# Spacing the blocks of the channel sub-layer's matmul operands 32 bytes further apart

## Chip, core and metric

The kernel runs on one core of a Trainium2 chip. The metric is the device time of one execution in microseconds (us). Before the change the median of three runs is 1179.09 us (1177.92 to 1179.61).

## What is computed

One layer of an encoder: a mixer sub-layer (neighbourhood attention and a two-way state-space branch), then the channel sub-layer, each followed by a layer norm. The change touches the channel sub-layer alone, which is a two-layer perceptron with a squared ReLU on 512 tokens, 1024 channels and 4096 hidden channels:

```python
def sq_relu_mlp(x, w1, w2):
    return jnp.square(jax.nn.relu(x @ w1)) @ w2

# in reference():
    h = layer_norm(DN_ALPHA * h + mix, ln1_g[l], ln1_b[l])
    h = layer_norm(DN_ALPHA * h + sq_relu_mlp(h, w_ff1[l], w_ff2[l]), ln2_g[l], ln2_b[l])
```

All data are float32.

## The kernel before

Every large product is done in three matmuls. Each operand is split into a rounded high part and the remainder (names ending in `h` and `l`), both of type float32r, and `mm3` (lines 404 to 406) adds high x high, low x high and high x low into one PSUM bank. A matmul has a **stationary** operand of 128 columns, which is loaded into the array as "weights", and a **moving** operand of 512 or 256 columns, which is streamed through. In the profile's names `ps_f<-h1Th,wh_f` the first name behind the arrow is the moving operand, the second the stationary one; the load of the stationary operand is a record of its own (PEld).

The channel sub-layer works on the hidden channels in four quarters of 1024 (`NQ`), each as eight tiles of 128 (`f`).

- **First product** (`ff1_half`, line 1458, and `ff1_tile`, line 1660). Moving: the normed tokens, transposed, as two tiles `h1Th` and `h1Tl` of eight blocks of 512 columns, one block for each 128 input channels. Stationary: a slab of `w_ff1` of 256 hidden channels, as eight blocks of 256 columns. For each of the eight blocks k there are three matmuls, with moving `h1Th`, `h1Th`, `h1Tl` of block k. The first four tiles of quarter 0 are done in two token halves (moving 256 columns, 192 matmuls in all), interleaved with the transposes that make `h1T`; their slabs are asked for with `shift=16`, that is 16 floats or 64 bytes into the tile (line 1500). All other tiles of the four quarters are 512 wide: 96 matmuls in quarter 0 and 192 in each other quarter, 672 in all.
- **Second product of quarters 0 to 2** (`ff2_strassen`, line 1561): 504 matmuls of 512 columns by Strassen's scheme. Its weights come by DMAs that add to what lies in the buffer (`w2r`, line 1570), and are split by ScalarE (line 1575) and VectorE (line 1576). Its operands are not moved by the change.
- **Second product of quarter 3** (`ff2`, line 1552). Stationary: the squares `gh` and `gl`, again eight blocks of 512 columns. Moving: blocks of 512 weights; 168 matmuls of 512 columns, and at the very end 48 of 256.

Slabs and split weights rotate through three pairs of buffers: two pairs of 2112 floats in pool `wp`, cut by `wide` (line 391), and one pair of 2048 floats in pool `w3` (`third`), cut by its own shape. `parts` (line 1522) deals them out in turn. `squares` (line 1687) makes the tiles of 4096 floats for the squares; `gh` and `gl` take the buffers of the first two quarters' squares, and the weights `rest` (line 1725) the third.

Below, the **place** of a block is the byte in its partition at which it begins, modulo 256. In the built program every tile of the channel sub-layer named above begins at a multiple of 256 bytes (`h1Th` at byte 70400, `wh` of pool `wp` at 36608 and 45056), and a block of 512 or 256 floats is 2048 or 1024 bytes long. So before the change every block has place 0, except the blocks of the slabs that are asked for with `shift=16`, which have place 64. The same holds in the mixer: `ps_z` (moving `wh_z`, `wl_z`) and the first `ps_x` slabs have place 64 by a shift, and most other operands place 0.

The order on each engine comes partly from a planner (the mixer) and partly from the order in which the code is written (the channel sub-layer).

Of the kernel before, what the change touches and what calls it, by code (L numbers as in the profile page):

```python
# [11 lines left out]
F32 = mybir.dt.float32  # L12
F32R = mybir.dt.float32r
# [6 lines left out]
P = 128  # L20
S = 512
D = 1024
NT = S // P
KD = D // P
# [333 lines left out]
def encoder_layer(ctx, tc, x, w_in, w_attn_br, w_ssd_br, w_o, w_ff1, w_ff2, pcols, rows64,  # L358
# [8 lines left out]
    wp = ctx.enter_context(tc.tile_pool(name="wp", bufs=2))  # L367
# [4 lines left out]
    def split_weights(parts, nk, ncol, name, hi, lo, eng=nc.vector, pool=None, after=None):  # L372


        st = (pool or wp).tile([P, nk, ncol], F32, tag="ws", name=f"ws_{name}")
        c = 0
        for src, r0, c0, n in parts:
            nc.sync.dma_start(
                st[:, :, c : c + n],
                src[r0 : r0 + nk * P, c0 : c0 + n].rearrange("(k p) c -> p k c", p=P),  # L380
            )
            c += n
        hk = nk // 2
        for i, k in enumerate((slice(0, hk), slice(hk, nk))):
            with tc.issue_after(after[i]) if after else ExitStack():
                nc.scalar.activation(hi[:, k], st[:, k], AF.Copy)  # L386
            (eng[i] if isinstance(eng, tuple) else eng).tensor_tensor(out=lo[:, k], in0=st[:, k], in1=hi[:, k].bitcast(F32),  # L387
                              op=ALU.subtract)
        return hi, lo

    def wide(t, nk, shift=0):

        return t[:, shift : shift + 2048].rearrange("p (k c) -> p k c", k=nk)

    def weights(parts, nk, ncol, name, eng=nc.vector, pool=None, after=None, shift=0):
        if pool:
            hi, lo = [pool.tile([P, nk, ncol], F32R, tag=n, name=f"{n}_{name}") for n in ("wh", "wl")]
        else:
            hi, lo = [wide(wp.tile([P, 2112], F32R, tag=n, name=f"{n}_{name}"), nk, shift)
                      for n in ("wh", "wl")]  # L400
        return split_weights(parts, nk, ncol, name, hi, lo, eng, pool, after)

    def mm3(o, lh, ll, rh, rl, start, stop):
        nc.tensor.matmul(o, lh, rh, start=start, stop=False)  # L404
        nc.tensor.matmul(o, ll, rh, start=False, stop=False)  # L405
        return nc.tensor.matmul(o, lh, rl, start=False, stop=stop)  # L406
# [89 lines left out]
    def slab(name, parts, nk, ncol, engs, shift=0):  # L496

        ws = plan.tile(f"ws_{name}", "ws", wp, [P, nk, ncol], F32)
        wh, wl = [plan.tile(f"{n}_{name}", n, wp, [P, 2112], F32R, lambda t: wide(t, nk, shift))
                  for n in ("wh", "wl")]  # L500
        c = 0
        keys = []
        for j, (src, r0, c0, n) in enumerate(parts):
            op("SP", 4.0 * n / ncol, lambda src=src, r0=r0, c0=c0, n=n, c=c: nc.sync.dma_start(
                ws()[:, :, c : c + n],
                src[r0 : r0 + nk * P, c0 : c0 + n].rearrange("(k p) c -> p k c", p=P)),
               r=[("behind", 0)], w=[(ws.name, j)], at=4.8 if name == "x0" else 4.4)
            keys.append((ws.name, j))
            c += n
        hk = nk // 2  # L510
        for i, (k, eng) in enumerate(zip((slice(0, hk), slice(hk, nk)), engs)):
            op("ACT", 1.06, lambda k=k: nc.scalar.activation(wh()[:, k], ws()[:, k], AF.Copy),
               r=keys, w=[(wh.name, i)])
            e, us = ("DVE", 1.24) if eng is nc.vector else ("POOL", 2.42)
            on = {"D": nc.vector, "P": nc.gpsimd}.get(ON.get(f"{wl.name}.{i}"), eng)
            op(e, us, lambda k=k, on=on: on.tensor_tensor(
                out=wl()[:, k], in0=ws()[:, k], in1=wh()[:, k].bitcast(F32), op=ALU.subtract),
               r=keys + [(wh.name, i)], w=[(wl.name, i)], lock=True)
        return wh, wl
# [828 lines left out]
    for tag, n in (("qf", 1), ("kf", 1), ("kh", 2), ("klz", 2), ("qs", 2)):  # L1348
        t = atp.tile([P, n, S], F32R, tag=tag, name=f"aTl_{tag}")
# [9 lines left out]
    for d2 in range(4):  # L1359
# [3 lines left out]
        tag = ("so", "mm")[d2 % 2]  # L1363
# [79 lines left out]
    apool.__exit__(None, None, None)  # L1443
    hpool.__exit__(None, None, None)
    fp = ctx.enter_context(tc.tile_pool(name="fp", bufs=1, reuse_waits="tile"))
    h1Th = fp.tile([P, KD, S], F32R, tag="h1Th", name="h1Th")
    h1Tl = fp.tile([P, KD, S], F32R, tag="h1Tl", name="h1Tl")
    acc = [fp.tile([P, D], F32, name=f"acc{t}") for t in range(NT)]
    h0.update({t: first_norm(t, acc[t], nc.gpsimd) for t in (2, 3)})

# [7 lines left out]
    def ff1_half(w1, j, ps, half):  # L1458

        c = slice(half * 256, (half + 1) * 256)  # L1460
        for k in range(KD):
            mm3(ps[:, c], w1[0][:, k, j * P : (j + 1) * P], w1[1][:, k, j * P : (j + 1) * P],
                h1Th[:, k, c], h1Tl[:, k, c], k == 0, k == KD - 1)

    def third(pool, name, shape=[P, KD, 256]):
        return [pool.tile(shape, F32R, tag=n, name=f"{n}_{name}") for n in ("wh3", "wl3")]
# [16 lines left out]
    for t2 in range(2):  # L1483
        toks = (2 * t2, 2 * t2 + 1)
        for c in range(2):
            cs = slice(c * 512, (c + 1) * 512)
            tag = ("mm", "so")[c]
# [8 lines left out]
        if t2:  # L1496

            early = []
            for s in range(2):
                w1 = weights([(w_ff1, 0, s * 256, 256)], KD, 256, f"f1_0_{s}", shift=16)  # L1500
                for j in range(2):
                    tag = ("so", "yd", "cb", "so")[2 * s + j]
# [12 lines left out]
    ffp = ctx.enter_context(tc.tile_pool(name="ffp", bufs=1, reuse_waits="tile"))  # L1515
# [3 lines left out]
             for i in range(2)]  # L1519
    turn = {"parts": 2, "raw": 0}  # L1520

    def parts(name, shape):

        turn["parts"] += 1
        if turn["parts"] % 3 == 0:
            return third(w3p, name, shape)
        return [wide(wp.tile([P, 2112], F32R, tag=n, name=f"{n}_{name}"), shape[1])
                for n in ("wh", "wl")]

    def raw(name):  # L1530
# [130 lines left out]
    def ff1_tile(fq, f, last):  # L1661

        s, j = f // 2, f % 2
        if fq == 0 and s < 2:
            w1, ps = early[f]
            ff1_half(w1, j, ps, 1)
        else:
            if j == 0:
                slab[0] = split_weights([(w_ff1, 0, fq * D + s * 256, 256)], KD, 256, f"f1_{fq}_{s}",
                                        *parts(f"f1_{fq}_{s}", [P, KD, 256]))  # L1670
            w1 = slab[0]
            ps = psx.tile([P, S], F32, tag="mm", bufs=BANKS["mm"], name=f"ps_f1_{fq}_{f}")
            for k in range(KD):
                mm3(ps, w1[0][:, k, j * P : (j + 1) * P], w1[1][:, k, j * P : (j + 1) * P],
                    h1Th[:, k, :], h1Tl[:, k, :], k == 0, k == KD - 1)
        rl = ffp.tile([P, S], F32, tag="rl", bufs=2, name=f"rl{fq}_{f}")
        nc.scalar.activation(rl, ps, AF.Relu)
        if last:
            nc.vector.tensor_tensor(out=rl, in0=rl, in1=ps, op=ALU.mult)
            nc.scalar.activation(gh[:, f, :], rl, AF.Copy)  # L1680
            return nc.vector.tensor_tensor(out=gl[:, f, :], in0=rl, in1=gh[:, f, :].bitcast(F32),
                                           op=ALU.subtract)
        return nc.scalar.activation(r2[fq][:, f, :], rl, AF.Square)

    slab = [None]

    def squares(name, dtype=F32):
        return ffp.tile([P, KD, S], dtype, tag="r2", bufs=3, name=name)

    r2 = [squares(f"r2_{fq}") for fq in range(2)]  # L1690
    for fq in range(2):
        for f in range(KD):
            ins = ff1_tile(fq, f, False)
            if fq == 1 and f == 0:
                begin = ins
            if fq == 0 and f == 4:

                for t in range(NT):
                    for i, o in ((0, ALU.mult), (1, ALU.add)):
                        aff = nc.gpsimd.tensor_tensor(out=acc[t], in0=acc[t], in1=row1[i], op=o)  # L1700
                        if i == 0:
                            tc.add_manual_dep(aff.ins, ins.ins.name, mybir.DependencyInfo(
                                mybir.DependencyClass.Sync, mybir.DependencyReason.DATA),
                                reason="behind the first channels")

    r2.append(squares("r2_2"))
    run = ff2_strassen(0, 0, r2[:2])
    for f in range(0, KD, 2):
        for _ in range(3):
            next(run)  # L1710
        ff1_tile(2, f, False)
        ff1_tile(2, f + 1, False)
    for _ in run:
        pass

    gh, gl = squares("gh", F32R), squares("gl", F32R)
    run = ff2_strassen(1, 2, r2[2:])
    for f in range(0, KD, 2):
        ff1_tile(3, f, True)
# [2 lines left out]
            next(run, None)  # L1722

    r0 = (NQ - 1) * D
    rest = ffp.tile([P, 2, 4, 512], F32R, tag="r2", bufs=3, name="w2_4")
    slabs = [[split_weights([(w_ff2, r0 + k0 * P, i * 512, 512)], 4, 512, f"f2_3_{i}_{k0}", *x)
              for k0, x in y] for i, y in enumerate((
                  ((0, [ffp.tile([P, 4, 512], F32R, tag="wr", bufs=2, name=f"w2{n}_0") for n in "hl"]),
# [86 lines left out]
```

## Time and profile before

| what | value |
|---|---|
| median of the runs | 1179.09 us |
| profiled execution, its own time | 1179.89 us |
| its span (first to last instruction) | 1178.1 us |
| TensorE clock granted, mean | 0.996 |
| first tile of the channel sub-layer's first product starts at | 832.0 us |
| last matmul of the kernel starts at | 1170.06 us |

The profile's page gives busy time by engine, then the chain of work that ended last, then groups of instructions. A matmul's duration overlaps that of the next, so the time of a matmul in a stream is the distance between two starts in the timeline, not its duration. Such a distance is called the **pitch** here. The timeline prints starts to 0.01 us, so a pitch is taken over many matmuls.

### The profile page before, as it was taken

How to read it: one execution, taken by the hardware profiler on the slowest of the kernel's cores; microseconds unless marked ns; L12 is line 12 of the kernel's file. 1: busy time of each engine (PE TensorE's matmuls, PEld its weight loads, DVE VectorE, ACT ScalarE, POOL GpSimd, SP SyncE). 2: the span in 40 equal slices, each digit the busy share in tenths (PEclk: the TensorE clock that was granted, in tenths of full speed). 3: DMA queues.
4: the chain of work that ended last, by engine and by line, in shares of the span. 5: the costliest groups of instructions: out<-in, count | busy, mean ns of one | idle time of the engine just before them, and what ended most of it. 6: DMA issues, size and time to landing. Idle time of an engine off the chain costs nothing.

```text
span 1178.1 us, 17062 instructions
## 1 busy us (share of the span) xinstructions
PE 1159.9 (98%) x6442; PEld 982.9 (83%) x6442; DVE 761.0 (65%) x1363; ACT 615.0 (52%) x1033; POOL 545.6 (46%) x588
## 2 busy tenths in 40 slices
PE   8999999999999999999999999999999999999997
PEld 8978797879888888888888888888988888878886
DVE  7757475676766665434788975556552666498856
ACT  6577583836365564524667773342263554365410
POOL 1168968778788767204667630016055131221000
PEclk9999999999999999999999999999999999999999
DMA  6353333333333342233423313543237986779511
GB/s 202 94 162 126 107 126 108 124 110 126 107 108 115 120 142 69 75 107 87 101 70 90 86 37 107 179 170 117 72 108 201 248 194 184 189 207 228 160 52 53
DMA packets 129409, 149.22 MB, mean 127 GB/s; under 512 B 22960, under 2 KB 101808, under 8 KB 129328
## 3 DMA queue, kind: packets, MB, share of 16 engines
q1 hardware_dynamic: 115696, 112.63, 30.8%
q0 software_dynamic: 13056, 34.61, 12.2%
q8 instruction: 50, 0.82, 0.3%
q10 hardware_dynamic: 576, 0.92, 0.2%
q14 instruction: 31, 0.25, 0.1%
HBM read 145.90 MB, written 2.23 MB: 126 GB/s over the span
## 4 chain that ended last, share of the span: by engine, by line
PE 83%; DMA 6%; DVE 5%; ACT 2%; issue 2%; POOL 2%; SPq 1%; DVEq 0%; POOLq 0%; ACTq 0%
PE ps_f L404 8%; PE ps_f L406 8%; PE ps_f L405 8%; PE ps_x L404 4%; PE ps_x L406 4%; PE ps_x L405 4%; PE ps_abr L1373 4%; PE ps_sbr L404 2%; DMA w2r<-in_w_ff 2%; PE ps_z L404 2%; PE ps_sbr L406 2%; PE ps_z L405 2%; PE ps_z L406 2%; PE ps_sbr L405 2%; PE ps_g L405 2%; PE ps_g L404 2%
## 5 line engine op out<-in xcount | busy, mean ns | idle before, releaser
L787 DVE SCALAR_TENSOR_TENSOR cv<-ps_x,pc,cv 128x511 f32<-128x511 f32 (+1 forms) x128 | 95.7, 748 | 24.7 <-ACT cv L779 21.4
L405 PE MATMUL ps_f<-h1Th,wl_f 128*128 128x512 f32 (+1 forms) x288 | 104.0, 365 | 0.0
L404 PE MATMUL ps_f<-h1Th,wh_f 128*128 128x512 f32 (+1 forms) x288 | 103.6, 365 | 0.0
L406 PE MATMUL ps_f<-h1Tl,wh_f 128*128 128x512 f32 (+1 forms) x288 | 102.0, 365 | 0.0
L1576 DVE TENSOR_TENSOR wl_f<-w2r,wh_f 128x1024 fp32r<-128x1024 f32 x42 | 49.9, 1221 | 64.4 <-ACT wh_f L1575 64.1
L404 PE MATMUL ps_z<-wh_z,hTh 128*128 128x256 f32 x256 | 75.2, 294 | 0.0
L405 PE MATMUL ps_z<-wh_z,hTl 128*128 128x256 f32 x256 | 71.5, 279 | 0.0
L406 PE MATMUL ps_z<-wl_z,hTh 128*128 128x256 f32 x256 | 71.5, 279 | 0.0
L1570 POOL DMA_DIRECT2D w2r<-in_w_ff x30 | 36.3, 1416 | 70.7 <-DMA w2r<-in_w_ff 45.7
L405 PE MATMUL ps_f<-wh_f,sql 128*128 128x512 f32 x168 | 65.3, 390 | 0.9 <-DVE sql L1576 0.9
L1575 ACT ACTIVATE wh_f<-w2r 128x1024 fp32r<-128x1024 f32 x42 | 42.6, 1052 | 44.0 <-DMA w2r<-in_w_ff 32.6
L404 PE MATMUL ps_f<-wh_f,sqh 128*128 128x512 f32 x168 | 65.3, 391 | 0.3 <-ACT sqh L1575 0.3
L406 PE MATMUL ps_f<-wl_f,sqh 128*128 128x512 f32 x168 | 65.3, 390 | 0.1
L1104 DVE TENSOR_TENSOR ysacc<-ps_sbr,ysacc 128x512 f32<-128x512 f32 x56 | 38.5, 689 | 37.5 <-PE ps_sbr L406 37.1
L404 PEld LDWEIGHTS ps_f<-h1Th,wh_f 128*128 128x128 f32 x288 | 53.9, 188 | 9.0
L405 PEld LDWEIGHTS ps_f<-h1Th,wl_f 128*128 128x128 f32 x288 | 53.9, 188 | 8.7
L387 DVE TENSOR_TENSOR wl_f<-ws_f,wh_f 128x1024 fp32r<-128x1024 f32 x36 | 47.2, 1348 | 20.5 <-ACT wh_f L386 20.4
L406 PEld LDWEIGHTS ps_f<-h1Tl,wh_f 128*128 128x128 f32 x288 | 52.8, 188 | 8.6
L404 PE MATMUL ps_x<-hTh,wh_bc 128*128 128x512 f32 (+1 forms) x144 | 56.7, 394 | 0.5 <-ACT hTh L614 0.5
L404 PE MATMUL ps_sbr<-yTh,wh_sbr 128*128 128x512 f32 x128 | 55.7, 435 | 0.7 <-ACT yTh L1081 0.4
L406 PE MATMUL ps_x<-hTl,wh_bc 128*128 128x512 f32 (+1 forms) x144 | 53.5, 371 | 1.9 <-DVE hTl L629 1.9
L404 PE MATMUL ps_x<-hTh,wh_x 128*128 128x512 f32 (+1 forms) x144 | 54.6, 379 | 0.0
(346 smaller groups left out, 3724.0 us busy)
## 6 DMA issues: line engine op xcount, KB each, us to landing
ws_f<-in_w_ff SPq DMA_DIRECT2D x20, 1024.0 KB
w2r<-in_w_ff POOLq DMA_DIRECT2D x18, 1024.0 KB, 7.9
bc<-acs_d SPq DMA_DIRECT2D x32, 512.0 KB
w2r<-in_w_ff POOLq DMA_DIRECT2D x30, 512.0 KB, 9.4
ws_bc<-in_w_in SPq DMA_DIRECT2D x16, 512.0 KB
ws_x<-in_w_in SPq DMA_DIRECT2D x8, 1024.0 KB
ws_z<-in_w_in SPq DMA_DIRECT2D x8, 1024.0 KB
ws_g<-in_w_in SPq DMA_DIRECT2D x8, 1024.0 KB
```

The lines of the kernel that those rows point to most:

```text
L387: (eng[i] if isinstance(eng, tuple) else eng).tensor_tensor(out=lo[:, k], in0=st[:, k], in1=hi[:, k].bitcast(F32), op=ALU.subtract)
L404: nc.tensor.matmul(o, lh, rh, start=start, stop=False)
L405: nc.tensor.matmul(o, ll, rh, start=False, stop=False)
L406: return nc.tensor.matmul(o, lh, rl, start=False, stop=stop)
L787: op("DVE", 0.75, lambda j=j, o=o, n=n: nc.vector.scalar_tensor_tensor(out=acc()[:, o], in0=ps()[:, n], scalar=tap(j), in1=acc()[:, o], op ...
L1104: op("DVE", 0.69, lambda d=d, ps=ps: nc.vector.tensor_tensor(out=ysacc[:, d, :], in0=ps(), in1=ysacc[:, d, :], op=ALU.add), r=[(ps.name, 0 ...
L1373: ins.append(nc.tensor.matmul(pss[j], u, v, start=k + p == 0, stop=k == KD - 1 and p == 2))
L1570: nc.gpsimd.dma_start(t, rows(i, n, c, k), accum_op=ALU.add)
L1575: nc.scalar.activation(hi[:, k], x, AF.Copy)
L1576: low = nc.vector.tensor_tensor(out=lo[:, k], in0=x, in1=hi[:, k].bitcast(F32), op=ALU.subtract)
```

## The change

Blocks of three kinds of operand get eight floats (32 bytes) of unused space behind each: `h1Th` and `h1Tl` (stationary partner unchanged), `gh` and `gl`, and those first-product slabs of quarters 2 and 3 that fall to the `wp` buffers. By the turn of `parts` that is two slabs, the second and third of quarter 2; the others of those quarters fall to the `w3` pair, which stays as it is. Block k of a spaced operand begins at place 32 k, so its eight blocks take the eight places 0, 32, ... 224. Tiles behind `h1T` move by multiples of 256 bytes.

```diff
-    def wide(t, nk, shift=0):
-
-        return t[:, shift : shift + 2048].rearrange("p (k c) -> p k c", k=nk)
+    def wide(t, nk, shift=0, pad=0):
+
+        n = 2048 // nk
+        return t[:, shift : shift + nk * (n + pad)].rearrange("p (k c) -> p k c", k=nk)[:, :, :n]
...
-    h1Th = fp.tile([P, KD, S], F32R, tag="h1Th", name="h1Th")
-    h1Tl = fp.tile([P, KD, S], F32R, tag="h1Tl", name="h1Tl")
+    h1Th, h1Tl = [fp.tile([P, KD, S + 8], F32R, tag=n, name=n)[:, :, :S] for n in ("h1Th", "h1Tl")]
...
-    def parts(name, shape):
+    def parts(name, shape, pad=0):
...
-        return [wide(wp.tile([P, 2112], F32R, tag=n, name=f"{n}_{name}"), shape[1])
+        return [wide(wp.tile([P, 2112], F32R, tag=n, name=f"{n}_{name}"), shape[1], 0, pad)
                 for n in ("wh", "wl")]
...
-                                        *parts(f"f1_{fq}_{s}", [P, KD, 256]))
+                                        *parts(f"f1_{fq}_{s}", [P, KD, 256], 8 * (fq >= 2)))
...
-    def squares(name, dtype=F32):
-        return ffp.tile([P, KD, S], dtype, tag="r2", bufs=3, name=name)
+    def squares(name, dtype=F32, pad=0):
+        t = ffp.tile([P, KD * (S + 8)], dtype, tag="r2", bufs=3, name=name)
+        return t[:, : KD * (S + pad)].rearrange("p (k s) -> p k s", k=KD)[:, :, :S]
...
-    gh, gl = squares("gh", F32R), squares("gl", F32R)
+    gh, gl = squares("gh", F32R, 8), squares("gl", F32R, 8)
...
-    rest = ffp.tile([P, 2, 4, 512], F32R, tag="r2", bufs=3, name="w2_4")
+    rest = squares("w2_4", F32R).rearrange("p (n k) s -> p n k s", n=2)
```

No instruction changes its position on any engine. The operations keep their number; eight of them, the splits of the two spaced slabs on ScalarE and VectorE, get a three-dimensional shape. On VectorE the rows around the first of these slabs (`wl_f1_2_1`, with the splits of Strassen weights ahead and behind) are, before:

```order
L1629 TENSOR_TENSOR acc2_7790<-acc2_7790,ps_f2_0_6_0_8935 128x512
L1629 TENSOR_TENSOR acc3_7791<-acc3_7791,ps_f2_0_6_1_8936 128x512
L387 TENSOR_TENSOR wl_f1_2_1_9170<-ws_f1_2_1_9171,wh_f1_2_1_9169 128x1024 x2
L1576 TENSOR_TENSOR sql_1_8349<-as_0_2_1_9126,sqh_1_8348 128x512
L1576 TENSOR_TENSOR sql_0_8347<-r2_1_8351,sqh_0_8346 128x512
```

and with the change:

```order
L1629 TENSOR_TENSOR acc2_7790<-acc2_7790,ps_f2_0_6_0_8935 128x512
L1629 TENSOR_TENSOR acc3_7791<-acc3_7791,ps_f2_0_6_1_8936 128x512
L387 TENSOR_TENSOR wl_f1_2_1_9170<-ws_f1_2_1_9171,wh_f1_2_1_9169 128x4x256 x2
L1576 TENSOR_TENSOR sql_1_8349<-as_0_2_1_9126,sqh_1_8348 128x512
L1576 TENSOR_TENSOR sql_0_8347<-r2_1_8351,sqh_0_8346 128x512
```

Only the shape of the slab's split differs. One wait is added: because tiles move, GpSimd's first operation on `acc3` (line 1402) now also waits for VectorE's last sum of line 1423, whose inputs lay where `acc3` now ends.

## The prediction

> **What bounds the kernel.** I read the page's busy shares and its chain first.
>
> ```profile
> PE 1159.9 (98%) x6442; PEld 982.9 (83%) x6442; DVE 761.0 (65%) x1363; ACT 615.0 (52%) x1033; POOL 545.6 (46%) x588
> PE 83%; DMA 6%; DVE 5%; ACT 2%; issue 2%; POOL 2%; SPq 1%; DVEq 0%; POOLq 0%; ACTq 0%
> ```
>
> TensorE is busy nearly always and is 83% of the chain. Next came the busy time by stretch, for the first product's 512-wide part (858.6 to 922.3), a stretch inside the third quarter, the second product of quarter 3, and its last 256-wide matmuls (PE, PEld, DVE, ACT, POOL, clock, DMA share, GB/s):
>
> ```profile
> 858.60:922.30 63.70, 63.70 (x283) 52.71 (x282) 25.24 (x20) 31.61 (x47) 33.39 (x18) 1.00 0.66 180
> 992.90:1039.60 46.70, 45.48 (x197) 36.22 (x195) 25.91 (x33) 21.61 (x29) 11.52 (x12) 1.00 0.80 181
> 1126.20:1164.30 38.10, 38.10 (x170) 31.56 (x169) 21.07 (x43) 0.88 (x3) 0.00 (x0) 1.00 0.07 28
> 1164.30:1170.10 5.80, 5.80 (x50) 5.76 (x48) 2.27 (x5) 0.00 (x0) 0.00 (x0) 1.00 0.23 90
> ```
>
> Outside the second row PE fills its stretch at full clock (1.00), so each nanosecond off a matmul's pitch there comes off the kernel. The second row is an exception. The chain of waits (start, length, work) leaves PE there:
>
> ```profile
> 992.92 0.24 PE ps_f L405
> ...
> 1017.96 12.61 DMA w2r<-in_w_ff
> 1030.59 1.07 ACT wh_f L1575
> ...
> 1038.44 1.14 DVE wl_f L1576
> 1039.62 0.50 PE ps_f L406
> ```
>
> From 993 to 1039.6 loads and splits of Strassen weights set the end, and PE waits for them. A faster matmul in that stretch only makes PE wait longer.
>
> **What a matmul costs by the places of its operands.** This carries the prediction. The stationary operand of matmul i+1 is loaded while matmul i streams, so I compare the place of a moving block with that of the next stationary one. Both at place 0, 512 wide, first and last of 52 consecutive starts in the timeline:
>
> ```profile
> 899.80 0.39 PE L406 MATMUL ps_f<-h1Tl,wh_f 128*128 128x512 f32 x1
> ...
> 911.36 0.39 PE L406 MATMUL ps_f<-h1Tl,wh_f 128*128 128x512 f32 x1
> ```
>
> 11.56 us / 51 = **226.7 ns**. Both at place 0, 256 wide, 45 starts at the end of the kernel:
>
> ```profile
> 1164.78 0.28 PE L404 MATMUL ps_f<-wh_f,gh 128*128 128x256 f32 x1
> ...
> 1170.06 0.28 PE L406 MATMUL ps_f<-wl_f,gh 128*128 128x256 f32 x1
> ```
>
> 5.28 us / 44 = **120.0 ns**. The difference is 106.7 ns for 256 columns, 0.417 ns a column. So 512 columns are 213.3 ns and 256 are 106.7 ns, and at both widths the same **13.3 ns** is left over. Next, the stationary block displaced by 64 bytes (`shift=16`), 31 starts in the early halves:
>
> ```profile
> 833.49 0.28 PE L404 MATMUL ps_f<-h1Th,wh_f 128*128 128x256 f32 x1
> ...
> 836.89 0.28 PE L404 MATMUL ps_f<-h1Th,wh_f 128*128 128x256 f32 x1
> ```
>
> 3.40 us / 30 = 113.3 ns: **6.7 ns** is left over. The moving block displaced by 64 bytes instead (`ps_z`), 21 starts:
>
> ```profile
> 163.61 0.28 PE L404 MATMUL ps_z<-wh_z,hTh 128*128 128x256 f32 x1
> ...
> 165.97 0.28 PE L406 MATMUL ps_z<-wl_z,hTh 128*128 128x256 f32 x1
> ```
>
> 2.36 / 20 = 118 ns: 11.3 ns left over. And both at place 0 with a stationary operand of only 64 columns (`ps_dt`):
>
> ```profile
> 20.91 0.28 PE L404 MATMUL ps_dt<-hTh,wh_dt 128*64 128x256 f32 x1
> ...
> 21.25 0.28 PE L404 MATMUL ps_x<-hTh,wh_bc 128*128 128x256 f32 x1
> ```
>
> 0.34 / 3 = 113 ns: again 6.7 ns. So the surcharge follows the size of the stationary operand (6.7 ns for 64 columns, 13.3 for 128) and its place relative to the moving one (13.3 at the same place, 6.7 to 11.3 when displaced), and at place 0 it does not follow the moving width. I read this as the two streams of reads meeting in the same part of the memory.
>
> **The change part by part.** With spaced `h1T`, block k begins at place 32 k while the stationary blocks stay at 0: seven eighths of the matmuls become displaced. With spaced `gh` and `gl` the same holds with the roles exchanged. In the two spaced slabs both operands are at 32 k, two of three matmuls stay in line and the third is off by 32; I count these 96 matmuls as unchanged.
>
> Displaced 512-wide matmuls outside the covered stretch 993 to 1039.6: quarter 0, 96 x 7/8 = 84; quarter 1, 192 x 7/8 = 168; quarter 2, its first two tiles, 48 x 7/8 = 42 (the next four tiles have the spaced slabs, and the last two lie in the covered stretch); quarter 3, 168; second product of quarter 3, 168 x 7/8 = 147. That is 609. What a displaced 512-wide matmul saves is shown by no run of rows. Its bounds: nothing (it has time to spare while weights load), and 13.3 ns (the surcharge goes). I take 6.7 ns, the step from 120.0 to 113.3, since those rows have the same engine, tile (`h1Th`) and operation as most of the 609; the `ps_z` step would give 2.
>
> - 512 wide: 609 x 6.7 ns = -4.1 us.
> - The last 256-wide matmuls: 48 x 7/8 = 42, x 6.7 = -0.3 us.
> - The early halves lose: all 192 had the place that gave 113.3 ns. Now block 2 is in line (24 x 6.7 ns = +0.2 us), block 0 keeps its place, and the other 144 lie between 113.3 and 120, so 0 to +1.0 us; I take +0.4 us in all, because part of these matmuls run among transposes at a longer pitch anyway.
> - The eight reshaped splits, bounded by nothing and one more operation each (1.2 us on VectorE, 1.05 on ScalarE): 0, since the rows below show VectorE idle 1.77 us and 4.05 us around the second slab.
>
> ```profile
> 978.67 2.36 DVE L1576 TENSOR_TENSOR wl_f<-w2r,wh_f 128x1024 fp32r<-128x1024 f32 x2 [4.05 <-ACT wh_f L1575]
> 983.40 2.36 DVE L387 TENSOR_TENSOR wl_f<-ws_f,wh_f 128x1024 fp32r<-128x1024 f32 x2 [1.77 <-ACT wh_f L386]
> ```
>
> - The added wait on GpSimd: VectorE's last sum of line 1423 starts at 791.07 and GpSimd's operation at 796.31, after its DMA, so 0. Without that cover it would delay `acc3`, which six more GpSimd operations separate from its use.
>
> ```profile
> 791.07 0.68 DVE L1423 TENSOR_TENSOR gt<-gt,gt 128x512 f32<-128x512 f32 x1
> 796.31 8.53 POOL L1402 TENSOR_SCALAR acc<-acc,ln_mv,ln_rs 128x1024 f32<-128x1024 f32 x2 [6.24 <-DMA acc<-in_x]
> ```
>
> Sum: -4.1 - 0.3 + 0.4 = -4.0 us. The profiled execution took 1179.89 us (span 1178.1 and 1.8 around it), 0.8 above the median of the runs, 1179.09. Put on the median, the time is 1179.1 - 4.0 = **1175.1 us**.
>
> The Trainium skill (TensorE: Matmul & The Clock Gate, "Back-to-back issue gap") gives an isolated gap of N/2.4 + 2.5 ns, 215.8 ns at N = 512. The rows here show 226.7, so by that rule at most 10.9 ns could go, an estimate of 6.6 us for 609 matmuls.
>
> **Rivals.**
>
> *The 512-wide matmul does not mind.* While it streams for 213 ns, the load of 128 columns has time to spare, and the surcharge may be the moving stream's own. For it: one 512-wide matmul (831.76) has a displaced load behind it (the first early half), and its pitch is as before:
>
> ```profile
> 831.53 0.39 PE L405 MATMUL ps_o<-wh_o,mgl 128*128 128x512 f32 x1
> 831.76 0.39 PE L406 MATMUL ps_o<-wl_o,mgh 128*128 128x512 f32 x1
> 831.98 0.28 PE L404 MATMUL ps_f<-h1Th,wh_f 128*128 128x256 f32 x1
> ```
>
> 0.22 us to the next start against 0.23: no 6.7 ns are seen, though it is a single one with a change of width behind it. Against it: the surcharge of 13.3 ns at both widths, and 6.7 with 64 columns. Time: 1179.1 - 0.1 + 0.4, **1179.4 us**. This is also where the change doesn't do what it says. The Trainium skill (TensorE: Matmul & The Clock Gate, "Step-by-step: what each phase is for") says that the array reads its moving and its stationary operand through two independent ports. By that rule places would not matter, and this rival would hold. The rows of 120.0 and 113.3 ns speak against it at 256 columns.
>
> *The whole surcharge goes* from displaced blocks: 609 x 13.3 = -8.1 us, -0.3 and +0.4: **1171.1 us**. Against it: no displaced row at full rate is below 113.3.
>
> *Slower.* Changing the place every third matmul keeps PE from its steady rhythm. After a change of shape the pitch is longer for a while:
>
> ```profile
> 845.81 0.40 PE L404 MATMUL ps_f<-h1Th,wh_f 128*128 128x512 f32 x1
> ...
> 846.74 0.38 PE L463 MATMUL tp_h<-cst,acc 128*128 128x128 f32 x2
> ```
>
> Four matmuls in 0.93 us are 232.5 ns each, 5.8 above the steady 226.7. If every displaced block paid that: 609 x 5.8 = +3.5 us, and +0.8 from the early halves: **1183.4 us**. It decides from the point where displaced blocks save less than 0.4 us / 609 = 0.7 ns each on the mean. Against it: in the 31 displaced rows the pitch is steady at 113.3.
>
> **How the numbers follow.** Forecast 0.44, no effect 0.27, whole surcharge gone 0.12, slower 0.17. 0.2% (2.4 us) is about what a measurement of this kernel can tell from no change. The forecast lies 1.6 us beyond that bound; with its saving between the `ps_z` step and 6.7 ns, about a tenth of it falls within 0.2%. Faster: 0.40 + 0.12 = 0.52; same: 0.04 + 0.25 = 0.29; slower: 0.17 + 0.02 = 0.19. The range reaches from 1170.5, below the case in which the surcharge goes, to 1181.5, above the one without effect; left out is most of the slower case. The likeliest side's own range is 1171 to 1177.
>
> **What would show it.** In the after profile, starts of 512-wide `ps_f<-h1Th` in quarter 1: 220 ns where k is not 0, 226.7 for block 0, so 24 matmuls of a tile take 5.30 us instead of 5.44. The four tiles with spaced slabs keep 226.7. The last 256-wide matmuls average 114 instead of 120; the early halves are slightly longer. If the spaced slabs' tiles gain as well, the place by itself matters and not the relative place. If all are at 226.7, the first rival holds; above 228, the slower one. The waits between 1031 and 1040 grow by some tenths of a us.

## The result

| | before | after |
|---|---|---|
| median of five runs | 1179.09 us | 1182.95 us |
| lowest to highest | 1177.92 to 1179.68 | 1181.42 to 1185.88 |
| profiled execution, its own time | 1179.89 us | 1183.31 us |
| its span | 1178.1 us | 1181.5 us |

The ratio is 1.0037, with a 95% interval of 1.0020 to 1.0053. The kernel became slower by 0.4%, and 1182.95 us lies beyond the range that was given (1170.5 to 1181.5).

This is the line of busy times in the page of the kernel after:

```profile
PE 1164.3 (99%) x6442; PEld 982.8 (83%) x6442; DVE 762.9 (65%) x1363; ACT 614.5 (52%) x1033; POOL 545.4 (46%) x588
```

The number of matmuls is the same, and TensorE is busy for 4.4 us longer (1159.9 before); the other engines changed by less than 2 us. The time was lost on TensorE itself. The timeline says in which stages. These are the starts of the same seven matmuls in the kernel before: the first early half, the third 512-wide tile of quarter 0, the first Strassen product, the first tile of quarter 3, the second product of quarter 3, the first 256-wide matmul at the end, and the 47th of those:

```profile
831.98 0.28 PE L404 MATMUL ps_f<-h1Th,wh_f 128*128 128x256 f32 x1
...
868.06 0.39 PE L404 MATMUL ps_f<-h1Th,wh_f 128*128 128x512 f32 x1
...
922.49 0.39 PE L404 MATMUL ps_f<-wh_f,sqh 128*128 128x512 f32 x1
...
1044.74 0.39 PE L404 MATMUL ps_f<-h1Th,wh_f 128*128 128x512 f32 x1
...
1126.34 0.39 PE L404 MATMUL ps_f<-w2h,gh 128*128 128x512 f32 x1
...
1164.42 0.28 PE L404 MATMUL ps_f<-wh_f,gh 128*128 128x256 f32 x1
...
1169.93 0.28 PE L405 MATMUL ps_f<-wh_f,gl 128*128 128x256 f32 x1
```

and in the kernel after (its lines are one higher):

```profile
831.25 0.28 PE L405 MATMUL ps_f<-h1Th,wh_f 128*128 128x256 f32 x1
...
868.26 0.40 PE L405 MATMUL ps_f<-h1Th,wh_f 128*128 128x512 f32 x1
...
924.06 0.40 PE L405 MATMUL ps_f<-wh_f,sqh 128*128 128x512 f32 x1
...
1046.24 0.39 PE L405 MATMUL ps_f<-h1Th,wh_f 128*128 128x512 f32 x1
...
1129.04 0.39 PE L405 MATMUL ps_f<-w2h,gh 128*128 128x512 f32 x1
...
1167.91 0.28 PE L405 MATMUL ps_f<-wh_f,gh 128*128 128x256 f32 x1
...
1173.36 0.28 PE L406 MATMUL ps_f<-wh_f,gl 128*128 128x256 f32 x1
```

Each stage's length, after minus before:

| stage | before | after | difference |
|---|---|---|---|
| early halves and first two 512-wide tiles | 36.08 | 37.01 | +0.93 |
| ten 512-wide tiles of quarters 0 and 1 | 54.43 | 55.80 | +1.37 |
| quarter 2, among Strassen products | 122.25 | 122.18 | -0.07 |
| quarter 3, among Strassen products | 81.60 | 82.80 | +1.20 |
| second product of quarter 3, 512 wide | 38.08 | 38.87 | +0.79 |
| last 256-wide matmuls (46 distances) | 5.51 | 5.45 | -0.06 |

That is +4.2 us. The first stage starts 0.7 us earlier in this execution, which leaves the 3.4 us by which the spans differ. Quarter 2 is a case of its own. From its first Strassen product to the start of its seventh tile (993.21 before, 995.29 after) it took 70.72 us before and 71.23 after, because its tiles became longer too. From there the chain runs through the loads of Strassen weights, and the first of these transfers took 1.0 us less in this execution. The row of before, then that of after:

```profile
998.97 9.63 DMA w2r<-in_w_ff
...
1001.06 8.60 DMA w2r<-in_w_ff
```

The rest of the quarter took 51.53 us before and 50.95 after, and 50.91 in a second execution of the kernel before (experiment 10). So the -0.07 does not show that the longer tiles cost nothing there; the loads hide it.

Now the pitch. Three pairs of rows of the kernel after: 96 matmuls of quarter 1, the 24 of one tile with a spaced slab, and 30 distances in the early halves, at the same matmuls as the 31 starts of before.

```profile
879.42 0.40 PE L405 MATMUL ps_f<-h1Th,wh_f 128*128 128x512 f32 x1
...
901.74 0.40 PE L405 MATMUL ps_f<-h1Th,wh_f 128*128 128x512 f32 x1
...
967.92 0.39 PE L405 MATMUL ps_f<-h1Th,wh_f 128*128 128x512 f32 x1
...
973.44 0.39 PE L405 MATMUL ps_f<-h1Th,wh_f 128*128 128x512 f32 x1
```

```profile
832.76 0.29 PE L405 MATMUL ps_f<-h1Th,wh_f 128*128 128x256 f32 x1
...
836.33 0.28 PE L405 MATMUL ps_f<-h1Th,wh_f 128*128 128x256 f32 x1
```

- Quarter 1: 22.32 us / 96 = **232.5 ns**, against 226.7. A tile of 24 takes 5.58 us instead of 5.44.
- A tile with a spaced slab: 5.52 / 24 = 230.0 ns.
- The second product of quarter 3 (1129.04 to 1167.91): 38.87 / 168 = 231.4 ns.
- The last 256-wide matmuls: 5.45 / 46 = 118.5 ns, against 120.0.
- The early halves: 3.57 / 30 = 119.0 ns, against 113.3.

So a matmul of 512 columns costs 5.8 ns more on the mean of quarter 1, where the forecast had a displaced one cost 6.7 ns less. It is the price that the slower rival named (232.5). What was open is the mechanism.

### The profile page after: what moved, and what is told of

It is laid out like the page before. It is cut to its first block, busy times and chain, and to the rows that moved or that the text cites. A ratio compares the mean times of both kernels' runs of the same rounds, so it can differ in the third digit from the quotient of the medians.

```text
span 1181.5 us, 17063 instructions
## 1 busy us (share of the span) xinstructions
PE 1164.3 (99%) x6442; PEld 982.8 (83%) x6442; DVE 762.9 (65%) x1363; ACT 614.5 (52%) x1033; POOL 545.4 (46%) x588
## 4 chain that ended last, share of the span: by engine, by line
PE 84%; DMA 5%; DVE 4%; issue 2%; ACT 2%; POOL 2%; SPq 1%; DVEq 0%; POOLq 0%; ACTq 0%
PE ps_f L407 8%; PE ps_f L405 8%; PE ps_f L406 8%; PE ps_x L405 4%; PE ps_x L407 4%; PE ps_x L406 4%; PE ps_abr L1374 4%; PE ps_sbr L405 2%; PE ps_sbr L407 2%; PE ps_sbr L406 2%; PE ps_z L405 2%; DMA w2r<-in_w_ff 2%; PE ps_z L406 2%; PE ps_z L407 2%; PE ps_g L407 2%; PE ps_g L405 2%
```

## The experiments

Three theories stood at the start. The relative place (R): the distance between a moving block and the stationary block that is loaded beside it sets the pitch. The change (C): what costs is that the place changes from block to block. The moving block's own place (M). All runs are told. Several have a single time. The runs of the kernel before that stand beside them reach from 1175.8 to 1180.1 us in one series (experiments 1 to 4) and from 1176.6 to 1184.7 in another (5, 6, 7 and 12). A single time therefore decides nothing here; the pitch does. Over the first four tiles of quarter 1 it is 226.7 ns in each of the six profiles that have all blocks in line there (two of the kernel before, two of `gh` and `gl` alone, experiments 9 and 12), and 232.5 in both that space `h1T` as the change does (the kernel after, and experiment 5). The diffs show the lines that matter; the arguments that carry a shift or a spacing through `parts` and `third` are left out.

### 1. Slabs displaced as a whole

Spacing is taken out. Each slab of the 512-wide first product begins at a place of its own and keeps it for all its blocks; the moving tiles stay at place 0.

```diff
-                                        *parts(f"f1_{fq}_{s}", [P, KD, 256]))
+                                        *parts(f"f1_{fq}_{s}", [P, KD, 256], 8 * ((4 * fq + s) % 8)))
```

> The kernel before, except that every whole slab of the first product is displaced as a block: all its eight blocks begin at one place, 32 x (4 fq + s mod 8), for quarter fq and slab s, while the moving blocks stay at place 0. So within a slab the relative place is constant, and over 14 slabs all eight distances occur. Theory R (what counts is the distance between the moving block and the stationary block that is loaded under it): the tiles of the one slab in line (quarter 2, slab 0) keep 5.44 us for 24 matmuls (226.7 ns each), and displaced slabs have a pitch of their own, some above 228 ns, on the mean about 232 as with the change (5.5 to 5.65 us a tile). Theory C (what costs is that the place changes from block to block): all slabs keep 226.7 ns, 5.44 us a tile.

One run: 1180.95 us. The timeline, with the first matmuls of the slabs at places 96, 128, 160, 192 and 224 (48 matmuls each) and the row that ends them; then a slab at place 0 (24):

```profile
867.48 0.39 PE L404 MATMUL ps_f<-h1Th,wh_f 128*128 128x512 f32 x1
...
878.72 0.39 PE L404 MATMUL ps_f<-h1Th,wh_f 128*128 128x512 f32 x1
...
889.87 0.39 PE L404 MATMUL ps_f<-h1Th,wh_f 128*128 128x512 f32 x1
...
901.08 0.40 PE L404 MATMUL ps_f<-h1Th,wh_f 128*128 128x512 f32 x1
...
912.08 0.40 PE L404 MATMUL ps_f<-h1Th,wh_f 128*128 128x512 f32 x1
...
923.27 0.39 PE L404 MATMUL ps_f<-wh_f,sqh 128*128 128x512 f32 x1
...
939.59 0.39 PE L404 MATMUL ps_f<-h1Th,wh_f 128*128 128x512 f32 x1
...
945.03 0.39 PE L404 MATMUL ps_f<-h1Th,wh_f 128*128 128x512 f32 x1
```

11.24, 11.15, 11.21, 11.00 and 11.19 us / 48 are 234.2, 232.3, 233.5, 229.2 and 233.1 ns; at place 0 it is 5.44 / 24 = 226.7. Places 32 and 64 gave 233 as well. Displacement costs without any change from block to block, and no distance is better than none.

### 2. The same with the moving tiles at place 96

```diff
+    h1Th, h1Tl = [fp.tile([P, KD * S + 64], F32R, tag=n, name=n)[:, 24 : 24 + KD * S].rearrange(
+        "p (k s) -> p k s", k=KD) for n in ("h1Th", "h1Tl")]
```

> As the run before it, with both moving tiles 96 bytes further on: the moving blocks are all at place 96. Theory R: the slabs at place 96 (quarter 0 slab 3, quarter 2 slab 3) are in line and have 226.7 ns, the slab at place 0 is not, and slabs with the same distance in the two runs have the same pitch within 1 ns. Theory M (the moving block's own place counts): all tiles of 512 columns are off 226.7, whatever their slab's place. Theory C: all keep 226.7.

One run: 1183.41 us. The slab at place 96, now in line, and the next one, at place 128:

```profile
868.91 0.39 PE L404 MATMUL ps_f<-h1Th,wh_f 128*128 128x512 f32 x1
...
879.80 0.39 PE L404 MATMUL ps_f<-h1Th,wh_f 128*128 128x512 f32 x1
...
890.99 0.40 PE L404 MATMUL ps_f<-h1Th,wh_f 128*128 128x512 f32 x1
```

10.89 / 48 = 226.9 ns, where the same slab had 234.2; then 11.19 / 48 = 233.1. The moving block's own place does not matter (M falls): each of the eight distances occurs in both runs, at different places, and has the same pitch in both within 1 ns, the 64 bytes of the quickest displaced slabs among them (229 ns in both). After these two runs I held R.

### 3. All of the first product spaced, each moving block in line with the next load

Every slab is spaced like `h1Th`, and `h1Tl` lies 32 bytes further on, so that the third matmul of a block stands at the place of the next block's slab. `gh` and `gl` are not spaced.

```diff
+    h1Th, h1Tl = [fp.tile([P, KD * (S + 8) + 64], F32R, tag=n, name=n)[:, i : i + KD * (S + 8)].rearrange(
+        "p (k s) -> p k s", k=KD)[:, :, :S] for i, n in ((0, "h1Th"), (8, "h1Tl"))]
...
+                                        *parts(f"f1_{fq}_{s}", [P, KD, 256], 8))
```

> The first product's moving and stationary blocks are all spaced by 32 bytes, in every slab of whole tiles, and the low moving tile begins 32 bytes further on, so that each moving block has the place of the stationary block that is loaded under it although all eight places are taken. The squares of quarter 3 lie as before the change. Theory R: 226.7 ns, 5.44 us a tile, and the kernel within 0.15% of the one before (only the early halves, whose slabs keep one place, lose some 0.7 us). Theory C: the pitch stays near 230 to 232 as with the change, and the kernel is 2.5 to 3.5 us slower than before.

Median of seven runs: 1181.95 us, ratio 1.0032 (1.0021 to 1.0044). Quarter 1, 96 matmuls:

```profile
879.58 0.40 PE L405 MATMUL ps_f<-h1Th,wh_f 128*128 128x512 f32 x1
...
901.90 0.40 PE L405 MATMUL ps_f<-h1Th,wh_f 128*128 128x512 f32 x1
```

22.32 / 96 = 232.5 ns, as with the change, though every moving block is in line with the load beside it. **R falls** as it stood. The first two matmuls of a block have everything in line and still take 230 and 227 ns in one block and 233 and 236 in the next. What a matmul costs depends on those ahead of it.

### 4. Only `gh` and `gl` spaced, and 5. only `h1Th` and `h1Tl` spaced

> Only the part of the change that spaces the squares of quarter 3; the first product lies as before. If the parts add up: 226.7 ns in all of the first product, and in the second product of quarter 3 the same 231.4 ns as with the whole change (11.11 us instead of 10.88 for 48 matmuls), +0.8 us in 168 matmuls, and the last 48 of 256 columns at 118 instead of 120. Theories R and C both expect this.

> The change without its parts on gh, gl and on the two slabs: only h1Th and h1Tl are spaced. If the parts add up: all 512-wide tiles of the first product at 5.56 to 5.60 us, the four tiles whose slabs were spaced too (5.52 with the whole change) among them; second product of quarter 3 at 226.7; span 2.5 to 3.2 us above the kernel before.

With `gh` and `gl` alone: 1178.45 us, the first product at 226.7, the second product of quarter 3 at 5.55 us for 24 (231.4 ns) as with the whole change. With `h1Th` and `h1Tl` alone: 1182.83 us, span 1181.1, all full tiles of quarter 1 at 5.58 us, the second product of quarter 3 at 226.7, and two tiles whose slab the whole change spaces at 5.56 and 5.58 instead of 5.52. Stage by stage the parts add up: most of the loss is `h1T`'s, 0.8 us is `gh`'s and `gl`'s.

### 6. Only the low moving tile displaced

The new theory: every change of place from one read to the next disturbs the stream, moving to stationary and back included, and the disturbance outlasts the matmul (the sequence theory). Here `h1Tl` lies 32 bytes on, so one matmul of three is displaced.

```diff
+    h1Th, h1Tl = [fp.tile([P, KD * S + 64], F32R, tag=n, name=n)[:, i : i + KD * S].rearrange(
+        "p (k s) -> p k s", k=KD) for i, n in ((0, "h1Th"), (8, "h1Tl"))]
```

> The low moving tile h1Tl as a whole 32 bytes on, all else of the first product at place 0. Two of three matmuls of a block stay in line with the load that runs beside them, the third is displaced by 32. Pair theory (a matmul is longer only when its own moving block and the next stationary block are out of line): per block 226.7, 226.7, 233.3, a tile of 24 in 5.49 us. Sequence theory (every change of place from one read to the next costs, and the cost lasts over the matmuls behind it, as in the run where the moving tiles followed the slabs): all three are longer, a tile in 5.55 to 5.60 us.

One run: 1180.93 us. Quarter 1, 96 matmuls:

```profile
879.03 0.39 PE L404 MATMUL ps_f<-h1Th,wh_f 128*128 128x512 f32 x1
...
901.43 0.39 PE L404 MATMUL ps_f<-h1Th,wh_f 128*128 128x512 f32 x1
```

22.40 / 96 = 233.3 ns. The median pitches of the three in a block are 232, 232 and 236: the two that are in line pay nearly as much as the displaced one. A price for each pair alone would have given 228.9 on the mean.

### 7. One jump in the middle of a tile

In quarters 0 to 2 the moving tiles and the slabs stand at place 0 in blocks 0 to 3 and at place 32 in blocks 4 to 7. In quarter 3 only the moving tiles jump. `Jump` is a helper that cuts a tile in two halves with so many floats between them.

```diff
+    h1Th, h1Tl = [Jump(fp.tile([P, KD * S + 64], F32R, tag=n, name=n), KD, S, 8) for n in ("h1Th", "h1Tl")]
...
+        return [Jump(pool.tile([P, 2112], F32R, tag=n, name=f"{n[:2]}_{name}"), KD, 256, 8) for n in tags]
```

> In quarters 0 to 2 blocks 0 to 3 of moving tiles and slabs stand at place 0 and blocks 4 to 7 at place 32, so everything is in line but the third matmul of blocks 3 and 7. In quarter 3 the slabs stay at place 0, so the last 12 matmuls of a tile are displaced by 32. Pair theory: 22 matmuls of 24 at 226.7, a tile in 5.45 to 5.46 us; quarter 3: the first twelve 226.7, the last twelve 233.3, a tile in 5.52. Sequence theory with a short memory: some 17 ns for each of two changes, a tile in 5.47 to 5.48, with the two or three matmuls behind each change long; with a long memory (over eleven matmuls): 5.55 to 5.60 in all quarters.

One run: 1183.31 us. One tile of quarter 1: the 6th matmul, the 12th (the last ahead of the jump), the 21st and the 24th.

```profile
887.44 0.39 PE L421 MATMUL ps_f<-h1Tl,wh_f 128*128 128x512 f32 x1
...
888.80 0.40 PE L421 MATMUL ps_f<-h1Tl,wh_f 128*128 128x512 f32 x1
...
890.87 0.39 PE L421 MATMUL ps_f<-h1Tl,wh_f 128*128 128x512 f32 x1
...
891.55 0.40 PE L421 MATMUL ps_f<-h1Tl,wh_f 128*128 128x512 f32 x1
```

Ahead of the jump 1.36 / 6 = 226.7 ns. The nine matmuls from the jump on take 2.07 / 9 = 230.0; one by one their medians are 235, 230, 224, 231, 236, 228, 232, 231 and 227. Then 0.68 / 3 = 226.7. Only the first of the nine is out of line. One change of 32 bytes disturbs the stream for about nine matmuls and costs some 34 ns. A tile, with two changes, takes 5.51 us instead of 5.44; in quarter 3, where the last twelve are displaced throughout, the two tiles of a slab take 5.52 and 5.56. The size of the recovery was under-expected (17 ns a change).

### 8. The same jump with 128 bytes

> As the run with one jump of 32 bytes between blocks 3 and 4, with 128 bytes in its place. Sequence theory: the same kind of recovery, some six to ten matmuls above 226.7 behind each change and 226.7 from there on; a tile of quarters 0 to 2 in 5.48 to 5.52 us; quarter 3, whose last twelve are displaced by 128 throughout, 5.52 to 5.56. Pair theory: 5.45 and 5.50.

One run: 1182.81 us. The 6th, 12th, 14th and 24th matmul of a tile of quarter 1:

```profile
888.06 0.39 PE L421 MATMUL ps_f<-h1Tl,wh_f 128*128 128x512 f32 x1
...
889.42 0.40 PE L421 MATMUL ps_f<-h1Tl,wh_f 128*128 128x512 f32 x1
...
889.88 0.39 PE L420 MATMUL ps_f<-h1Th,wl_f 128*128 128x512 f32 x1
...
892.15 0.40 PE L421 MATMUL ps_f<-h1Tl,wh_f 128*128 128x512 f32 x1
```

1.36 / 6 = 226.7, then 233 and 231 ns, then 2.27 / 10 = 227.0. The tile takes 5.46 us, less than the sequence theory expected: after a change of 128 bytes only one further matmul is disturbed. The length of the recovery depends on the size of the change, which the theory did not foresee. In quarter 3 the tiles take 5.51 and 5.53 us (5.52 to 5.56 expected).

### 9. 256 bytes between the blocks of `h1Th`

```diff
+    h1Th = fp.tile([P, KD, S + 64], F32R, tag="h1Th", name="h1Th")[:, :, :S]
```

> The blocks of h1Th lie 256 bytes further apart, so every block keeps place 0 (h1Tl, slabs, gh and gl as before). If spacing as such costs (another stride, other rows of the memory): tiles of the first product at 5.55 to 5.60 us, as with 32 bytes on h1Tl alone, and 1182 to 1183 us. If only the place modulo 256 counts: all at 5.44 us, and within 0.1% of the kernel before.

Median of ten runs: 1178.16 us, ratio 1.0001 (0.9990 to 1.0011). Quarter 1, 96 matmuls:

```profile
877.58 0.39 PE L404 MATMUL ps_f<-h1Th,wh_f 128*128 128x512 f32 x1
...
899.34 0.39 PE L404 MATMUL ps_f<-h1Th,wh_f 128*128 128x512 f32 x1
```

21.76 / 96 = 226.7 ns. This spacing is free; the place modulo 256 is what costs.

The seventh tile of the quarter took 5.57 us, and it shows something that no experiment was made for. TensorE waits there once for ScalarE. The load behind that wait, then the second matmul of the tile and the tenth:

```profile
910.20 0.19 PEld L404 LDWEIGHTS ps_f<-h1Th,wh_f 128*128 128x128 f32 x1 [0.25 <-ACT rl L1677]
...
910.54 0.40 PE L405 MATMUL ps_f<-h1Th,wl_f 128*128 128x512 f32 x1
...
912.39 0.39 PE L404 MATMUL ps_f<-h1Th,wh_f 128*128 128x512 f32 x1
```

1.85 / 8 = 231 ns, with all blocks in line; one by one the eight pitches are 233, 236, 224, 231, 235, 229, 233 and 231, and from there on it is 226.7 again. The series is nearly that behind the jump of 32 bytes in experiment 7. The kernel before has it too: behind a wait in quarter 2 (matmuls from 1007.54 to 1009.63) nine pitches average 232 ns, and 226.7 follows. So a wait alone does what a change of place by 32 bytes does: the stream leaves a steady pace and finds it again only after eight or nine matmuls.

### 10. The kernel before, and 11. the `gh` and `gl` kernel, profiled again

> The kernel before, unchanged, profiled a second time. The question is the 113.3 ns of the early halves, from which the forecast took its 6.7 ns. If the places alone set that pitch: a median of 113 to 114 again. If the same places have two pitches and history decides between them: 113 to 114 or 117 to 118, as the run with gh and gl alone showed, whose early halves stand at the same places. The last 256-wide matmuls, in line throughout, at 120.0 and the 512-wide at 226.7 in either case.

> The kernel with gh and gl alone spaced, profiled again and timed. In its first profile the early halves ran at 117 to 118 ns, although every operand of theirs has the address that it has in the kernel before (113 to 114 in two profiles). If the execution decides between the two pitches: either may come, and 113 to 114 shows it. If something in this program decides: 117 to 118 again. Second product of quarter 3 at 5.55 us for 24 again (+0.8 us in all), the last 256-wide at 118, and the time within 0.1% of the kernel before, 0.07% being what the tiles give.

The kernel before again: 1178.24 us, and the same 31 starts of the early halves (832.45 to 835.85) at 113.3 ns. The `gh` and `gl` kernel, median of twelve runs: 1179.47 us, ratio 1.0009 (0.9995 to 1.0024), its second product of quarter 3 at 231.4 again. Its early halves, first profile and second, at the same matmuls:

```profile
833.08 0.28 PE L405 MATMUL ps_f<-h1Th,wh_f 128*128 128x256 f32 x1
...
836.62 0.28 PE L405 MATMUL ps_f<-h1Th,wh_f 128*128 128x256 f32 x1
```

```profile
833.22 0.28 PE L405 MATMUL ps_f<-h1Th,wh_f 128*128 128x256 f32 x1
...
836.62 0.28 PE L405 MATMUL ps_f<-h1Th,wh_f 128*128 128x256 f32 x1
```

3.54 / 30 = 118.0 ns in one execution and 3.40 / 30 = 113.3 in the other, from the same program. So 113.3 is not what these places cost; it is one of two paces that they can fall into. It is the more frequent one: the same places occur in experiments 1, 9 and 12, at 113.3 each time, which makes six executions of seven. The run of experiment 1 was on the same chip as the execution with 118.0, so the chip alone does not decide.

### 12. `ps_z` at another distance

> The kernel before, with the slabs of ps_z shifted by 48 floats instead of 16, so that moving blocks stand at place 192 and the stationary at 0 (distance 192 instead of 64). If the distance sets the pitch at 256 columns too: 113 to 114 ns as in the early halves and the first ps_x slabs instead of 118; 768 matmuls x 4.7 ns = 3.6 us where TensorE sets the end, less where the mixer waits for others: 1175 to 1178 us. If distance 192 falls into the second pitch of 117 to 118 that the run with gh and gl alone had in its early halves: 1178 to 1179.

A try for a version better than both kernels. Median of twelve runs: 1179.40 us, ratio 0.9998 (0.9981 to 1.0015). The median pitch of `ps_z` is 117 ns where it was 118, but this median hides two paces. Two stretches of the one profiled execution, 30 distances each:

```profile
47.92 0.28 PE L406 MATMUL ps_z<-wl_z,hTh 128*128 128x256 f32 x1
...
51.32 0.28 PE L406 MATMUL ps_z<-wl_z,hTh 128*128 128x256 f32 x1
...
165.66 0.28 PE L404 MATMUL ps_z<-wh_z,hTh 128*128 128x256 f32 x1
...
169.20 0.28 PE L404 MATMUL ps_z<-wh_z,hTh 128*128 128x256 f32 x1
```

3.40 / 30 = 113.3 ns and 3.54 / 30 = 118.0, at the same places. About a third of the 768 matmuls stand in groups that ran at 113 to 114 ns; in the kernel before, with 64 bytes in place of 192, every such group had 118. So the distance of the early halves did bring their 113.3 with it, but only in part: at this distance a stream falls into one of the two paces, and both occur within one execution. No version of this study is faster than the kernel before.

## Why the prediction was wrong, point by point

- **What bounds the kernel** held. Where PE fills its stretch, its pitch came through to the end (ten tiles: 10 x 0.14 = 1.4 us, measured +1.37). In quarter 2 the tiles ahead of 993 cost 0.5 us, and from there on the loads set the end, as was said; what the longer tiles cost behind them can't be told from how long the transfers took.
- **The step that failed** is "I take 6.7 ns, the step from 120.0 to 113.3". It sized the main term at -4.1 us; the three open stages of 512-wide tiles measured 1.37 + 1.20 + 0.79 = +3.4. It failed twice over. The step was carried from 256 columns to 512, where no distance tried went below 226.7 (experiment 1): displaced matmuls cost 5.8 ns more instead of 6.7 less. And 113.3 is not the price of the places: at the same distance streams ran at 113.3 or at 118.0 (experiments 10 to 12).
- **The reading** "the two streams of reads meeting in the same part of the memory" is refuted at 512 columns: the same place for both is the best case, at place 0 and at place 96 alike. The 113 ns for 64 stationary columns, from which a part of it came, rested on three distances printed to 0.01 us, which leaves 110 to 117.
- **The spaced slabs' tiles** were to keep 226.7, because two matmuls of three are in line. They took 230.0. Being in line does not help a matmul just behind a change (experiments 3, 6 and 7).
- **The last 256-wide matmuls**: 118.5 ns, not 114; -0.1 us instead of -0.3. **The early halves**: of the +0.9 us of their stage, two 512-wide tiles account for 2 x 0.14; the rest, about +0.65, stands against +0.4. Part of it may be the second pace and not the change: in the first profile of `gh` and `gl` alone, whose halves ran at 118 ns with their operands unmoved, this stage took 36.46 us instead of 36.08.
- **The terms at zero** held: the reshaped splits took 1.22 us on VectorE and 1.05 to 1.06 on ScalarE, as before, and the channel sub-layer did not start late behind GpSimd's added wait (831.25, before 831.98).
- **The slower rival** was right in size: 232.5 ns, from four matmuls behind a change of width, and 1183.4 us against a measured 1182.95. That the two pitches agree to the digit is luck, since displaced streams took from 229.2 to 234.2. Its mechanism held in part. That the stream falls out of a steady rhythm, and recovers only over some matmuls, is what experiments 3, 6 and 7 show, and the tile behind a wait in experiment 9. That the place must change from block to block is not needed: a constant distance between the two streams does the same (experiment 1). The argument against it, the steady 113.3 of displaced rows, was of the wrong width and of one pace out of two.
- **The rival without effect** leaned on a single matmul (831.76), whose pitch can be read to 10 ns only. Its -0.1 us for the last 256-wide matmuls stands without a reason beside the -0.3 of the forecast; they measured -0.06. The rule cited with it (the Trainium skill, TensorE: Matmul & The Clock Gate, "Step-by-step: what each phase is for": two independent ports) does not agree with these runs if it is read so that start addresses cannot matter: 226.7 ns at one place, 232.5 at the eight.

What stays open: what in the memory or the array keeps the steady pace, why a change of 32 bytes is felt for nine matmuls, like a wait, and one of 128 bytes for two, and what decides between 113.3 and 118 ns.

## What to carry to other kernels

A pitch read at one width is evidence for that width alone; here the rows at 512 columns, even four of them, were worth more than 31 at 256. Let the blocks that a long stream of 512-wide matmuls reads, moving and stationary, begin at the same byte modulo 256; 256 bytes of padding behind each block cost nothing here. And read what follows the waits in the old profile: the kernel before already showed what a stream costs that has lost its pace, 232 ns. One more execution would not have warned of the 113.3, which came back in five of six; another stream at the same distance did (experiment 12).

## What was not expected of the hardware

- At 512 columns of float32r, 226.7 ns when all blocks begin at the same place modulo 256; 229.2 to 234.2 when the stationary ones are displaced by a constant, least when moving minus stationary is 64 bytes (229.2).
- A wait of TensorE has the same aftermath as a change of place by 32 bytes: with all blocks in line, the eight matmuls behind it average 231 ns before 226.7 returns.
- One change of place for both operands costs about 34 ns over nine matmuls at 32 bytes, and about 11 ns over two at 128 bytes (233 and 231 against 226.7).
- At 256 columns it is the other way round: 120.0 in line, 113.3 to 119 displaced. With moving minus stationary at 192 bytes there are two paces, 113.3 and 118.0, for the same program, and for the same operands within one execution.
